# Round 1's first retention head: both projection quads in turn, in seven block products, with a changed release of the state work, in a split-precision conv and retention trunk

## The chip, the cores and the metric

One core of one Trainium2 chip. The metric is the device time of one execution in microseconds; for the kernel before it is the median of three runs. A program profiled once gives the trace that the readings below come from.

## The reference

One mixer layer on 2048 positions of 1024 features, with 16 learned meta tokens ahead of them. Every position is normalised and multiplied by one matrix of 1024 x 4096, and the result is cut into eight groups of 512: four feed a gated convolution of width three, four a retention with four heads of 128. Both halves are gated, joined and multiplied by a second matrix of 1024 x 1024, and a residual and a final normalisation follow.

```python
h = jnp.concatenate([meta_b, x], axis=1)
hn = rms_norm(h, norm_g)
proj = jnp.einsum('bld,de->ble', hn, w_in)
cx, cb, cc, cg, q, k, v, rg = jnp.split(proj, N_PROJ, axis=-1)
conv_out = short_conv_branch(cx, cb, cc, conv_w) * jax.nn.silu(cg)
qf = rotary(q.reshape(shp).astype(jnp.float32), pos) * (RET_HEAD_DIM ** -0.5)
kf = rotary(k.reshape(shp).astype(jnp.float32), pos)
ret = head_group_norm(retention_chunkwise(qf, kf, vf), ret_norm_g)
ret_out = ret.astype(h.dtype) * jax.nn.silu(rg)
mixed = jnp.concatenate([conv_out, ret_out], axis=-1)
return h + jnp.einsum('ble,ed->bld', mixed, w_out)
```

In the retention, each chunk of 128 positions has scores of q with k, multiplied by a decay and applied to v, and adds what q reads from a running state of 128 x 128, which is multiplied by a chunk decay and gets k^T v of each chunk. The state starts from the meta tokens.

## The kernel before, in words

**Precision and products.** Every operand of the large products is split into a high and a low part (`split`, L113): ScalarE (ACT) writes the high part as a cast, VectorE (DVE) subtracts it from the source for the low part. A product of two blocks is then three matmuls per 128 rows: low weights by high data (`wl`, `mh`), high by low (`wh`, `ml`), high by high. A matmul of the large kind has a 128 x 128 weight and 512 columns.

**Quads.** The work of TensorE (PE) is cut into quads: four output blocks of 128 x 512 from 2 x 2 blocks of weights and of data. `quad` (L252) makes one in seven block products of twelve matmuls each (Strassen's scheme in Winograd's form: seven sums of weights, seven sums of data, and sums of the outputs). `quad_plain` (L309) makes it in eight, without sums. The sums of the weights for products 2 to 5 are built by GpSimd (POOL) in `stationary` (L143): L131 and L128 on tiles `ra` and `sa`, each followed by the split, a cast `wh` on ACT (L119) and a low part `wl` on DVE (L120). Only three pairs `wh`, `wl` are held at a time (`RING`).

**Rounds and units.** Two rounds of 1024 positions. A round has eight units of two quads each: units 0 to 3 are retention heads (`head`, L787: one quad for K and V, one for Q and the gate RG), 4 to 7 are convolution groups (`conv_group`, L646). Round 0 takes them in the order 4, 0, 1, 2, 3, 5, 6, 7, round 1 in the order 0 to 7; then `output` makes the second product. In round 1 the first head has the plain quad for K and V (L309), because the data's sums are still on their way from DRAM (`prepared`, L224), and the quad in seven for Q and RG.

**What a head does behind its quads.** Outputs of a quad come by `take`: a copy `tc` of a bank by ACT (L259), a sum from bank and copy by DVE (`kv`, `qg`, L128). K and Q are rotated in place by four DVE operations (`rotary`, L742 to L745). V and K are taken apart into 16-bit planes (`part`), transposed by a DMA and put together again (`join`, `join_keys`, ACT). Then follow, for two halves j of four chunks each: products of v and kd that update the state (PE at L895, DVE at L898), the scores (PE at L908), their decay `pm` (DVE at L910), the outputs (v by pm at L918, state by q at L919), statistics and normalisation. The turned outputs (`apart`) come back from a DMA one unit later and are multiplied with the gate (DVE at L948).

**The meta tokens.** In round 0, sixteen small matmuls (L506, `meta_products`) multiply the raw weights `ra` of the *next* unit by the meta tokens; four ACT copies (L512) bring them to `mk`. Since POOL builds the weight sums in the same `ra` tiles, it waits for them. `meta_state` (L525) then makes a head's starting state: two DVE sums, three products and one sum on `mk` (L128, L532, L533), one matmul (L536), one copy.

**What sets the order.** Each engine works through its queue in the order in which it was given. The order comes from a scheduler that simulates the program, and from `tc.issue_after(x)`, which keeps what is written inside it behind instruction x in the order. `head` ends with two such places: `next(sums)` (a step that makes sums for the next round) and `meta_state` are put behind `queried[0]`, the first rotation of q, which comes behind product 1 of the second quad. Its second rotation comes behind product 5.

**The row product.** In `take` of `conv_group` (L664 to L676), the gated input u is multiplied by a row factor, `u<-u,rr`, on DVE (L663).

## Time and profile before

| what | us |
|---|---|
| median of three runs (864.99 to 865.04) | 865.0 |
| the profiled execution | 865.38 |
| its span, first to last instruction | 863.6 |
| PE busy | 853.8 |
| DVE busy | 675.1 |
| ACT busy | 499.7 |
| POOL busy | 280.0 |
| round 1's first head, plain quad and quad in seven | 354.0 to 405.7 |

Times in the views are counted from the start of the span. A row of the chain or of a timeline gives start, length, engine, what is written from what is read, the line, and how many instructions the row groups (a small matmul in full precision counts twice). "Idle before" stands in brackets with what ended it. A matmul's own length of 0.39 us is longer than its pitch, since matmuls overlap; the pitch counts.

### The profile page before, as it was taken

The page shows a single profiled execution, that of the slowest core. Times are in us where ns is not written, and L with a number is a line of the kernel's source. Part 1 is how long each engine was busy: PE and PEld are TensorE (multiplying, and loading weights), DVE is VectorE, ACT ScalarE, POOL GpSimd, SP SyncE. Part 2 cuts the span into 40 slices and gives each one's busy share as a digit, 9 for nine tenths or more (in the row PEclk, how much of TensorE's full clock was granted, in tenths as well). Part 3 has the DMA queues.
Part 4 walks back from the last instruction along what each step waited for, and adds up shares of the span by engine and source line. Part 5 has one row for each costly group of instructions (what it writes and reads, how often), then busy time and mean ns, then how long its engine had stood idle before and what let it go on. Part 6 is the DMA issues. An engine that isn't in the chain of part 4 may idle for free.

```text
span 863.6 us, 12850 instructions
## 1 busy us (share of the span) xinstructions
PE 853.8 (99%) x4216; PEld 705.5 (82%) x4216; DVE 675.1 (78%) x1207; ACT 499.7 (58%) x901; POOL 280.0 (32%) x224
## 2 busy tenths in 40 slices
PE   9999999999999999999999999999999999999996
PEld 6778888878887778888888888888888878888885
DVE  6798989889897977979677787976655699766553
ACT  7775648474845554948284757544433475555553
POOL 0032332422245554110000002341312154777773
PEclk9999999999999999999999999999999999999999
DMA  9736257565777744966275657547334584455441
GB/s 323 245 122 171 91 148 213 143 190 184 183 239 236 244 147 159 340 197 171 74 183 175 162 190 173 180 135 256 99 120 122 199 326 146 159 172 178 150 134 74
DMA packets 141331, 154.43 MB, mean 179 GB/s; under 512 B 59920, under 2 KB 77904, under 8 KB 141264
## 3 DMA queue, kind: packets, MB, share of 16 engines
q1 hardware_dynamic: 140688, 153.21, 57.6%
q8 instruction: 33, 0.54, 0.3%
q10 hardware_dynamic: 576, 0.40, 0.1%
q14 instruction: 34, 0.28, 0.1%
HBM read 101.14 MB, written 39.85 MB: 163 GB/s over the span
## 4 chain that ended last, share of the span: by engine, by line
PE 95%; DVE 2%; DMA 1%; ACT 1%; issue 1%; ACTq 0%; POOLq 0%; DVEq 0%; SPq 0%
PE pj L252 76%; PE pj L333 5%; PE pj L309 5%; PE ms L919 2%; PE ms L908 2%; PE ms L918 2%; PE ms L895 2%; PE ms L506 1%; DMA w<-in_w_out 1%; DMA ra<-in_w_in 0%; DVE wl L120 0%; DVE qg L948 0%; DVE x L205 0%; PE ms L381 0%; DVE u L663 0%
## 5 line engine op out<-in xcount | busy, mean ns | idle before, releaser
L252 PE MATMUL pj<-mh,wl 128*128 128x512 f32 x1008 | 395.6, 392 | 1.9 <-DVE wl L120 1.1
L252 PE MATMUL pj<-mh,wh 128*128 128x512 f32 x1008 | 393.2, 390 | 0.0
L252 PE MATMUL pj<-ml,wh 128*128 128x512 f32 x1008 | 392.8, 390 | 0.0
L119 ACT CAST wh<-ra 128x512 fp32r<-128x512 f32 x229 | 142.2, 621 | 256.2 <-PE pj L252 220.0
L120 DVE TENSOR_TENSOR wl<-ra,wh 128x512 fp32r<-128x512 f32 x229 | 185.8, 813 | 64.2 <-ACT wh L119 62.3
L252 PEld LDWEIGHTS pj<-mh,wl 128*128 128x128 f32 x1008 | 189.3, 188 | 42.8 <-ACT wh L119 1.7
L252 PEld LDWEIGHTS pj<-mh,wh 128*128 128x128 f32 x1008 | 189.2, 188 | 39.3
L252 PEld LDWEIGHTS pj<-ml,wh 128*128 128x128 f32 x1008 | 189.3, 188 | 38.3
L131 POOL TENSOR_TENSOR ra<-ra 128x512 f32<-128x512 f32 x44 | 68.3, 1553 | 80.9 <-PE ms L506 38.7
L931 POOL TENSOR_TENSOR rp<-rs,neg_half 128x4 f32<-128x4 f32 x16 | 18.8, 1173 | 150.3 <-DVE rs L128 150.2
L259 ACT COPY tc<-pj 128x512 f32<-128x512 f32 x108 | 62.6, 580 | 0.1
L128 POOL TENSOR_TENSOR sa<-ra 128x512 f32<-128x512 f32 x22 | 32.5, 1480 | 55.8 <-DMA ra<-in_w_in 28.7
L994 DVE TENSOR_TENSOR yo<-pj,yo 128x512 f32<-128x512 f32 (+1 forms) x33 | 21.9, 672 | 24.3 <-PE pj L252 16.1
L131 POOL TENSOR_TENSOR ra<-sa,ra 128x512 f32<-128x512 f32 x22 | 30.4, 1380 | 30.9 <-DVE wl L120 21.1
L1005 POOL TENSOR_TENSOR z<-yo,final_g 128x512 f32<-128x512 f32 x16 | 26.4, 1651 | 19.5 <-DVE yo L994 19.5
L128 POOL TENSOR_TENSOR yo<-yo,tc 128x512 f32<-128x512 f32 x18 | 28.0, 1560 | 6.6 <-ACT tc L259 6.5
L128 DVE TENSOR_TENSOR tc<-pj,tc 128x512 f32<-128x512 f32 x26 | 17.8, 686 | 15.4 <-PE pj L252 15.3
L935 DVE TENSOR_SCALAR pm<-ms,mv,rp 128x128 f32<-128x128 f32 x64 | 21.9, 403 | 10.1 <-POOL rp L931 10.0
L663 POOL TENSOR_TENSOR c<-c,tc 128x512 f32<-128x512 f32 x12 | 18.2, 1516 | 34.2 <-ACT tc L693 21.8
L663 POOL TENSOR_TENSOR c<-c,rr 128x512 f32<-128x512 f32 x12 | 19.3, 1609 | 27.1 <-DVE c L713 17.0
L581 DVE SCALAR_TENSOR_TENSOR c<-u,conv_w,c 128x512 f32<-128x512 f32 x32 | 25.2, 831 | 2.3 <-POOL u L572 1.2
L123 DVE SCALAR_TENSOR_TENSOR ml<-x,gain,mh 128x512 fp32r<-128x512 f32 x32 | 22.6, 745 | 4.7 <-ACT mh L122 4.7
(168 smaller groups left out, 1214.5 us busy)
## 6 DMA issues: line engine op xcount, KB each, us to landing
ra<-in_w_in SPq DMA_DIRECT2D x111, 256.0 KB, 2.9
ra<-sums_a SPq DMA_DIRECT2D x52, 256.0 KB, 2.9
x<-in_xT SPq DMA_DIRECT2D x48, 256.0 KB, 5.0
sums_a<-ra SPq DMA_DIRECT2D x42, 256.0 KB, 2.1
w<-in_w_out SPq DMA_DIRECT2D x32, 256.0 KB, 5.0
ra<-mixed SPq DMA_DIRECT2D x32, 256.0 KB, 2.7
yo<-in_x SPq DMA_DIRECT2D x32, 256.0 KB, 4.3
ra<-in_x SPq DMA_DIRECT2D x16, 256.0 KB, 3.3
```

Of the source, the lines that this page charges most:

```text
L119: nc.scalar.copy(out=hi, in_=src)
L120: lowered[0] = eng.tensor_tensor(out=lo, in0=src, in1=hi.bitcast(F32), op=ALU.subtract)
L123: nc.vector.scalar_tensor_tensor(out=lo, in0=src, scalar=scale, in1=hi.bitcast(F32), op0=ALU.mult, op1=ALU.subtract)
L128: eng.tensor_tensor(out=out, in0=a, in1=b, op=ALU.add)
L131: eng.tensor_tensor(out=out, in0=a, in1=b, op=ALU.subtract)
L252: nc.tensor.matmul(bank, a[:, ks], b, start=first and kt == 0 and n == 0, stop=kt == KH - 1 and n == 2, skip_group_check=not first,)
L259: copied[0] = nc.scalar.copy(out=c, in_=bank)
L309: nc.tensor.matmul(banks[i], a[:, ks], b, start=half + kt + n == 0, stop=half == 1 and kt == KH - 1 and n == 2,)
L333: nc.tensor.matmul(banks[n][i], a[:, ks], b, start=half + kt + s == 0, stop=half == 1 and kt == KH - 1 and s == 2,)
L581: nc.vector.scalar_tensor_tensor(out=c, in0=u[:, tap : tap + HB], scalar=conv_w[:, g, tap : tap + 1], in1=c, op0=ALU.mult, op1=ALU.add)
L663: eng.tensor_tensor(out=out, in0=a, in1=b, op=ALU.mult)
L1005: nc.gpsimd.tensor_tensor(out=ys[i][j], in0=y, in1=final_g[:, j * HB : (j + 1) * HB], op=ALU.mult)
```

## The change

Four things are changed.

1. Round 1's first head. A new `quads` makes both quads in turn: product 0 of K/V, product 0 of Q/RG, product 1 of K/V and so on, seven each (168 matmuls in place of 180). The weights of both come from generators (`weights_in_turn`) that load, cast and split one weight at a time in that order; a product's successor is asked for when the pair is issued. The data come by `moving_in_turn`: blocks, then the sums in the order 1, 0, 2, block B22, sum 3, as steps between the products. The sum T3 is split ahead of the two first rotations, which are put off (`turns`); B22 and T4 stand behind low parts of weights (`leads`). K's and V's transposes are no longer held back (`to_cross` is gone).
2. In round 0, `conv_group`'s row product for j = 0 stands behind the low part of the quad's fifth weights (`fifth`), where work of a head before it is still waiting.
3. In `take_queries`, the rotation is noted in `queried` only for j = 1.
4. `next(sums)` and `meta_state` stand behind `queried[-1]` in place of `queried[0]`. This holds for all heads of round 0 as well.

```diff
+    def quads(ws, w, m, takes, between=()):
+        between = iter(between)
+        banks = [[None, None] for _ in ws]
+        copies = [None for _ in ws]
...
+        for i in range(7):
+            for n in range(len(ws)):
+                if i < 2:
+                    banks[n][i] = ps_proj()
+                product(n, i, banks[n][i in (1, 3, 5)], i in (0, 1, 3))
+            w = [next(a, None) for a in ws[:1]]
+            leads[0] = lowered[0]
+            w += [next(a, None) for a in ws[1:]]
...
+            next(between, idle)()
...
+    def weights_in_turn(n, r):
+        for load in w_loads(n, r, in_line):
+            a = raw()
+            load(a)
+            yield weight_parts(a)
...
+        behind_head = r == 0 and len(waiting[1]) + len(waiting[0]) > 0
...
-                mul(nc.vector, s, s, rr2[j])
+                with queued((fifth[0],) if behind_head and j == 0 else ()):
+                    mul(nc.vector, s, s, rr2[j])
...
-                rotary(d, tables[j])
-                queried.append(turned[0])
+                if j == 0 and len(first):
+                    turns.append(lambda: rotary(d, tables[j]))
+                else:
+                    rotary(d, tables[j])
+                if j:
+                    queried.append(turned[0])
...
+            steps = [
+                first[1], lambda: turn_first(early[0]), fourth, fifth_pair, lambda: turn_first(leads[0]), split_values,
+                lambda: split_keys(1),
+            ]
+            quads(*first[0], m, (take_keys, take_queries), steps)
+            join_keys(0)
+            join(1)
+            weigh(1)
+            join(0)
+            weigh(0)
+            join_keys(1)
...
-        with tc.issue_after(queried[0].ins):
+        with tc.issue_after(queried[-1].ins):
             next(sums, None)
         if blocks[1]:
-            with tc.issue_after(queried[0].ins):
+            with tc.issue_after(queried[-1].ins):
                 meta_state(h, blocks[1], rot)
```

The order of PE in round 0, from head 1 to head 2, before: the head's starting state, the next head's meta products and the first state update stand right behind product 6's matmuls (the first row), and the next unit's product 0 follows (the last row).

```order
L252 MATMUL pj<-mh_461,wl 128x512
L252 MATMUL pj<-ml_462,wh 128x512
L252 MATMUL pj<-mh_461,wh 128x512
L536 MATMUL ms<-mk 128x128
L506 MATMUL ms<-ra,meta_s 16x128 x16
L895 MATMUL ms<-v,kd 128x128 x4
L252 MATMUL pj<-mh_126,wl 128x512
```

After, the same place: these are the last matmuls of the next unit's product 1 (rows of L274, which is the old L252; L607, L577, L1002, L1015, L1025 and L1026 are the old L536, L506, L895, L908, L918 and L919).

```order
L274 MATMUL pj<-ml_223,wh 128x512
L274 MATMUL pj<-mh_222,wh 128x512
L607 MATMUL ms<-mk 128x128
L577 MATMUL ms<-ra,meta_s 16x128 x16
L1002 MATMUL ms<-v,kd 128x128 x8
L1015 MATMUL ms<-qg,kv 128x128 x4
L1025 MATMUL ms<-v,pm 128x128
L1026 MATMUL ms<-state_84,qg 128x128
L1025 MATMUL ms<-v,pm 128x128
L1026 MATMUL ms<-state,qg 128x128
L1025 MATMUL ms<-v,pm 128x128
L1026 MATMUL ms<-state,qg 128x128
```

The block moved behind two products of the next unit, in one piece, and the scores with the first outputs moved up to it; behind the rows shown come the rest of the outputs, the second scores and the next unit's product 2.

The order of DVE in round 0, from head 0 to head 1, before: the operations on `mk` follow the first rotation of q (whose last operation is the first row).

```order
L745 TENSOR_TENSOR qg<-qg,rot 128x512
L128 TENSOR_TENSOR mk<-mk 16x128 x2
L533 TENSOR_TENSOR mk<-mk,mr 16x128
L532 TENSOR_TENSOR mk<-mk,mr 16x64 x2
L120 TENSOR_TENSOR wl<-ra,wh 128x512
L128 TENSOR_TENSOR mk<-mk 16x128
L128 TENSOR_TENSOR qg<-pj,tc 128x512
L837 TENSOR_TENSOR qg<-qg,rr 128x512
```

After: here the second rotation of q begins the rows (L821 to L824 are the old L742 to L745, L671 is the old L594, L604 and L603 the old L533 and L532).

```order
L821 TENSOR_TENSOR rot<-qg,rot_t 64x512
L822 TENSOR_TENSOR rot<-qg,rot_t 64x512
L908 TENSOR_TENSOR qg<-pj,rr 128x512
L823 TENSOR_TENSOR qg<-qg,rot_t 128x512
L824 TENSOR_TENSOR qg<-qg,rot 128x512
L671 TENSOR_TENSOR c<-c,rr 128x512 x2
L128 TENSOR_TENSOR mk<-mk 16x128 x2
L671 TENSOR_TENSOR c<-c,cb 128x512 x2
L604 TENSOR_TENSOR mk<-mk,mr 16x128
L603 TENSOR_TENSOR mk<-mk,mr 16x64 x2
L671 TENSOR_TENSOR c<-c,cb 128x512 x2
L128 TENSOR_TENSOR mk<-mk 16x128
```

The operations on `mk` moved behind the second rotation and between the products on c, which belong to the unit before.

The order of DVE in round 0 at conv unit 6's first quad, before (the row of L663 is the row product):

```order
L120 TENSOR_TENSOR wl<-sa,wh 128x512
L948 SCALAR_TENSOR_TENSOR qg<-apart,ret_g,qg 128x512
L128 TENSOR_TENSOR u<-pj,tc 128x512
L948 SCALAR_TENSOR_TENSOR qg<-apart,ret_g,qg 128x512
L663 TENSOR_TENSOR u<-u,rr_360 128x512
L120 TENSOR_TENSOR wl<-ra,wh 128x512 x3
L128 TENSOR_TENSOR ss<-ss 128x4
```

After:

```order
L120 TENSOR_TENSOR wl<-sa,wh 128x512
L1055 SCALAR_TENSOR_TENSOR qg<-apart,ret_g,qg 128x512
L128 TENSOR_TENSOR u<-pj,tc 128x512
L1055 SCALAR_TENSOR_TENSOR qg<-apart,ret_g,qg 128x512
L120 TENSOR_TENSOR wl<-ra,wh 128x512
L741 TENSOR_TENSOR u<-u,rr_360 128x512
L120 TENSOR_TENSOR wl<-ra,wh 128x512 x2
L128 TENSOR_TENSOR ss<-ss 128x4
```

One `wl`, the low part of the fifth weights, moved ahead of the row product (the old L663, now L741).

## The prediction

> **What bounds the kernel now.** I read the page first, then PE's waits, then the chain of work that ended last.

> ```profile
> span 863.6 us, 12850 instructions
> PE 853.8 (99%) x4216; PEld 705.5 (82%) x4216; DVE 675.1 (78%) x1207; ACT 499.7 (58%) x901; POOL 280.0 (32%) x224
> PEclk9999999999999999999999999999999999999999
> ```

> TensorE (PE) is busy for 99% of the span at the full granted clock. A matmul taken out is worth its own time, and a new wait on PE is paid in full. PE's waits hold one entry above 1 us inside the units:

> ```profile
> PE pj L252 <- DVE wl L120: 1.1, 1, 1.1
> ```

> The chain through round 1's first head (K/V quad at L309, Q/RG quad at L252) is matmuls without a gap:

> ```profile
> 354.03 5.44 PE pj L252 x24
> ...
> 370.58 16.09 PE pj L309 x71
> 386.67 19.04 PE pj L252 x84
> 405.71 0.89 PE ms L895 x8
> ```

> 84 matmuls take 19.04 us, 0.2267 us each, and L309 runs at the same pitch (16.09/71). A product of twelve is 2.72 us.

> **Part 1: seven products for eight in round 1's first head.** 96 + 84 matmuls become 84 + 84: 12 x 0.2267 = -2.72 us. What covers the new work is the slack of the other engines. The window of the two old quads (columns: length, then busy PE, weight loads, DVE, ACT, POOL):

> ```profile
> 354.00:405.70 51.70, 51.70 (x231) 42.81 (x230) 45.09 (x72) 38.32 (x66) 3.46 (x2) 1.00 0.76 244
> ```

> The K/V quad gains three low parts of weights and three sums on DVE, at 0.6 to 0.7 us each (rows below), about 4 us: 45.1 + 4 = 49.1 in a window of 51.7 - 2.7 = 49.0. DVE just fits; ACT, with three casts and three copies more (some 3.6 us), has room. Two quads in turn give each weight two products (5.44 us) of lead, and the rotations are put off, so DVE can slide. I count no stall, with 0 to +2 us as bounds: nothing in the trace makes it a gain, and if the cover is gone PE waits for a low part of one weight, priced as in part 2 at 1 to 2 us.

> **Part 2: the row product.** Columns: start, length, what, idle before it.

> ```profile
> 294.62 0.39 PE L252 MATMUL pj<-mh,wh 128*128 128x512 f32 x1
> 296.08 0.47 PE L252 MATMUL pj<-mh,wl 128*128 128x512 f32 x1 [1.07 <-DVE wl L120]
> ```

> ```profile
> 293.54 1.79 DVE L663 TENSOR_TENSOR u<-u,rr 128x512 f32<-128x512 f32 x1
> 295.25 1.88 DVE L120 TENSOR_TENSOR wl<-ra,wh 128x512 fp32r<-128x512 f32 x3
> ```

> In conv unit 6 DVE runs the row product ahead of the fifth weights' low part, and PE starts 296.08 - 294.62 - 0.23 = 1.23 us late. The new order puts the low part first: it can start at 293.54 instead of 295.25, 1.71 us sooner, which covers the 1.23. I take -1.2; bounds 0 (something else ends the wait) and -1.24.

> **Part 3: what `queried` moves in round 0.** The change appends only the second rotation of q and ties `meta_state` and `next(sums)` to it. That holds for every head, not only round 1's first. The order shows the result: in round 0, for heads 0, 1, 2 and 3, PE's block "meta state, 16 meta products, v by kd, scores" now stands behind products 0 and 1 of the next unit, directly ahead of product 2. Before, it was spread from product 5 on:

> ```profile
> 90.59 0.41 PE ms L536 x2
> 91.01 0.56 PE ms L506 x16
> 91.57 2.99 PE pj L252 x12
> 94.55 0.56 PE ms L506 x16
> 95.11 1.09 PE ms L895 x8
> ...
> 101.21 0.89 PE ms L895 x8
> 102.10 0.89 PE ms L908 x8
> ...
> 141.01 1.00 PE ms L506 x32
> ```

> Gain: where the meta products were in two pieces (heads 0 and 2) they cost 2 x 0.56 + (2.99 - 2.72) = 1.39 us, in one piece 1.00. Twice 0.39 is -0.8 us (bounds 0 and -0.8).

> Cost: what had other matmuls to hide behind now stands at one place, where PE itself waits. Behind the meta products the block holds only 1.09 + 0.89 + 0.89 = 2.87 us of PE work before product 2.

> *Head 0 to 1, the wait for `mk`.* PE is through product 5 at 90.59; 36 matmuls later, 8.16 us, it stands at the block: 98.7. The prices of DVE's rows there:

> ```profile
> 94.56 0.69 DVE L742 TENSOR_TENSOR rot<-qg,rot_t 64x512 f32<-64x512 f32 x1
> 95.27 1.82 DVE L743 TENSOR_TENSOR rot<-qg,rot_t 64x512 f32<-64x512 f32 x1
> 97.11 0.69 DVE L837 TENSOR_TENSOR qg<-pj,rr 128x512 f32<-128x512 f32 x1
> 97.72 0.28 DVE L898 SCALAR_TENSOR_TENSOR state<-state,ms 128x128 f32<-128x128 f32 x1
> ...
> 100.41 1.28 DVE L594 TENSOR_TENSOR c<-c,rr 128x512 f32<-128x512 f32 x2
> 101.61 0.28 DVE L898 SCALAR_TENSOR_TENSOR state<-state,ms 128x128 f32<-128x128 f32 x1
> ```

> ```profile
> 85.35 0.47 DVE L128 TENSOR_TENSOR mk<-mk 16x128 f32<-16x128 f32 x2
> ...
> 86.33 0.69 DVE L120 TENSOR_TENSOR wl<-ra,wh 128x512 fp32r<-128x512 f32 x1
> 86.94 0.27 DVE L128 TENSOR_TENSOR mk<-mk 16x128 f32<-16x128 f32 x1
> ```

> From 94.56 on, DVE has in its new order, counted from start to start: two rotation halves 1.42; gate by row factor 0.61, rotation's product 0.60 and sum 0.71; c by rr, two, 1.20; four products c by cb at the same pitch, 2.40; the mk operations 0.98 and 0.27. Together 8.2, so mk is there at about 102.7 and PE waits 4.0 us (3.7 to 4.3: each of the ten operations may be some 0.03 us off).

> *Head 0 to 1, product 2.* Its weights (third in line) are built by POOL from tiles that the meta products still read, and DVE must first finish what the block feeds:

> ```profile
> 95.26 1.28 POOL L131 TENSOR_TENSOR ra<-ra 128x512 f32<-128x512 f32 x1 [13.84 <-PE ms L506]
> 96.61 1.62 POOL L131 TENSOR_TENSOR ra<-sa,ra 128x512 f32<-128x512 f32 x1
> ```

> ```profile
> 95.21 1.06 ACT L512 COPY mk<-ms 16x128 f32<-16x128 f32 x4 [1.13 <-PE ms L506]
> 98.27 0.62 ACT L119 CAST wh<-ra 128x512 fp32r<-128x512 f32 x1 [0.82 <-POOL ra L131]
> 99.63 0.59 ACT L259 COPY tc<-pj 128x512 f32<-128x512 f32 x1
> ```

> By POOL: meta products' end 95.11 to the cast 98.27 is 3.16, cast 0.62, low part 0.69: 4.5. By ACT and DVE: mk copies 0.10 + 1.06, copy tc 0.59, then kv sum 0.67, state 0.28, two rotation halves 1.40, state 0.28, low part 0.69: 5.0. Against 2.87 of PE work the wait is 2.2 us. POOL runs beside it, and the row 95.27 shows what that does: 1.82 us for a rotation half whose twin took 0.69. One such meeting adds 1.1, two 2. I take 3.0 (2.2 to 4.2). [...]

> *Heads 1 to 2 and 2 to 3.* Here even the outputs of j = 0 (v by pm, state by qg) stand in the block, so PE waits for pm:

> ```profile
> 197.29 0.74 DVE L948 SCALAR_TENSOR_TENSOR qg<-apart,ret_g,qg 128x512 f32<-128x512 f32 x1
> 197.95 0.27 DVE L898 SCALAR_TENSOR_TENSOR state<-state,ms 128x128 f32<-128x128 f32 x1
> ...
> 198.81 0.68 DVE L910 SCALAR_TENSOR_TENSOR pm<-ms,causal 128x512 f32<-128x512 f32 x1
> 199.41 0.67 DVE L128 TENSOR_TENSOR kv<-pj,tc 128x512 f32<-128x512 f32 x1
> ```

> mk copies and tc 1.75, kv 0.67, state 0.27, rotation half 0.70, gate 0.74, other half 0.69, state 0.2, pm 0.68: with overlaps at the seams about 5.5; less 2.87 is 2.65 each. One meeting with POOL makes it 3.75. I take 3.3 each (2.65 to 3.75).

> *Head 3 to conv unit 5.* mk copies 1.16, DVE's mk work of the conv unit 0.74, states 0.7, u's sum 0.6, gate 0.7, pm 0.68: 4.6 less 2.87; I take 2.3 with part of a meeting (1.7 to 2.8).

> Sum of waits: 4.0 + 3.0 + 3.3 + 3.3 + 2.3 = +15.9, bounds 12.9 and 18.8.

> **The sum.** -2.7 - 1.2 - 0.8 + 15.9 = +11.2. The profiled execution took 865.38 us (its span and 1.8 outside); the median of the runs is 865.0, so the execution stands 0.4 above it, and the same step on the median gives 876. Bounds: 12.9 - 4.8 = +8.1 (873) to 18.8 - 2.7 + 0 + 2 - 0.8 = +17.3 (882).

> **Rivals.**
> 1. *Faster: the waits are covered.* Mechanism: the mk and pm chains are ready when PE gets there. It decides at the point where mk is done before 98.7 and the chain behind the meta products takes under 2.87 us. For it: before, these steps never made PE wait. Against: then about thirty full matmuls stood between scores and their use, now none. Time: 865.0 - 4.8 = 860.2.
> 2. *Half of it.* DVE fills PE's first wait with work that I counted behind it, and each later wait shrinks: +8 - 4.8 = +3, 868 (866.8 to 873).
> 3. *The clock.* Idle time lowers PE's granted clock. The only longer idle in the trace is the start:

> ```profile
> 0.99 4.45 PE L1070 MATMUL ms<-warm 128*128 128x512 bf16 x10 [0.99 <-DVE warm L1062]
> ```

> Ten matmuls take 0.445 us each, twice the later 0.2267: a cold stretch costs 2.2 us. After one wait of 4.0 that is 878; after all four of 3 us and more, 885. Against: after the wait of 1.07 us PEclk is unchanged. [...]
> 4. *Same.* Waits of about 5 us in all cancel the gains: 863.3 to 866.7.

> **Chances.** 0.2% is 1.7 us, about what a measurement of this kernel can tell from no change. Waits as summed 0.62; clock 0.10; half 0.08; covered 0.16; same 0.04. So slower 0.80, same 0.04, faster 0.16. Predicted: 876, the likeliest case, alone 873 to 882. The range runs from 864 to 882: it leaves out the covered case and the far end of the clock's.

> **What would show it.** In the new profile: no PE gap between 354 and 406 (part 1), with the next head's first small matmuls 2.7 us nearer to the first head's start; no wait of PE on wl near conv unit 6 (part 2); in round 0 four times a PE wait on mk, wl or pm directly ahead of a third product, 2 to 4 us each and two at head 0 to 1 (part 3). Wrong it is if PE's waits in round 0 sum to under 5 us, or if the first waits of round 1's first head exceed 2 us.

## The result and the profile after

The changed kernel takes 887.2 us (median; 886.6 to 887.8) against 865.0 before: 22.2 us slower, ratio 1.0253 (95% interval 1.0240 to 1.0266). The direction and the place were as forecast, the size was double: 876 was predicted, with 882 as the upper end of the range.

The page of the kernel after, with the lines that answer to those of before:

```profile
span 884.8 us, 12809 instructions
PE 859.6 (97%) x4204; PEld 711.6 (80%) x4204; DVE 688.0 (78%) x1209; ACT 498.8 (56%) x901; POOL 275.3 (31%) x224
PEclk9999899998999999999999999999999999999999
```

PE has twelve matmuls fewer and yet is busy 5.8 us longer, and two of the forty digits of the granted clock have fallen. So there are two costs: idle time, and matmuls that run slowly. The idle time is in PE's waits (us in total, times, longest):

```profile
PE ms L1025 <- DVE pm L1017: 8.0, 2, 4.0
PE ms L607 <- DVE mk L128: 3.6, 1, 3.6
PE ms L1025 <- ACT wh L119: 2.9, 1, 2.9
PE pj L274 <- DVE wl L120: 1.9, 1, 1.9
...
PE pj L274 <- ACT wh L119: 0.7, 1, 0.7
```

The first four rows are the five waits that the prediction named, 16.4 us together. The third row's wait is also one of v by pm; the page lists a cast as its last releaser.

The chain from head 0 to head 1 shows both costs in one place:

```profile
101.99 0.21 DVE mk L128
102.20 0.04 issue
102.25 0.79 PE ms L607 x2
103.04 1.91 PE ms L577 x32
104.95 0.02 issue
104.97 0.26 ACT mk L583
...
106.05 0.59 ACT tc L281
106.64 0.02 issue
106.67 0.69 DVE kv L128
107.36 0.20 DVE state L1005
107.58 0.69 DVE rot L821
108.28 1.68 DVE rot L822
109.98 0.29 DVE state L1005
110.27 0.61 DVE wl L120
110.88 0.04 issue
110.93 5.73 PE pj L274 x24
```

mk comes at 102.20, forecast 102.7. Behind the block stands the path that was added up by hand (mk copies, copy tc, kv, state, two rotation halves, state, low part), with one half at 1.68 us, beside a POOL operation (107.73 to 109.41), where the other took 0.69. But the matmul on mk takes 0.79 us, before 0.41, and the 32 records of the meta products 1.91 us, before 1.00: the granted clock is 0.50 there. The windows behind the long waits give the granted clock (the column behind the five engines):

```profile
102.25:104.00 1.75, 1.75 (x22) 1.32 (x26) 0.00 (x0) 0.27 (x1) 0.00 (x0) 0.50 0.95 268
104.00:106.00 2.00, 2.00 (x25) 1.53 (x14) 0.00 (x0) 0.99 (x4) 0.98 (x1) 0.50 0.10 27
106.00:108.00 2.00, 2.00 (x14) 2.00 (x13) 1.30 (x3) 0.94 (x3) 1.84 (x3) 0.63 0.35 131
```

```profile
162.00:164.00 2.00, 1.93 (x9) 1.96 (x10) 2.00 (x4) 0.00 (x0) 0.00 (x0) 0.52 0.59 206
164.00:165.50 1.50, 1.50 (x9) 1.50 (x9) 1.50 (x4) 0.00 (x0) 0.00 (x0) 0.50 0.77 239
```

```profile
214.80:217.00 2.20, 2.19 (x10) 2.20 (x11) 2.20 (x4) 0.00 (x0) 0.00 (x0) 0.50 0.60 203
217.00:219.00 2.00, 2.00 (x12) 2.00 (x11) 1.33 (x5) 0.00 (x0) 0.17 (x1) 0.50 0.73 174
219.00:221.00 2.00, 2.00 (x10) 1.84 (x10) 2.00 (x6) 0.00 (x0) 1.92 (x2) 0.72 0.42 130
```

```profile
267.30:269.00 1.70, 1.69 (x10) 1.70 (x11) 1.70 (x4) 0.02 (x1) 0.00 (x0) 0.68 1.00 310
269.00:271.00 2.00, 2.00 (x12) 2.00 (x11) 2.00 (x7) 0.00 (x0) 0.00 (x0) 0.50 0.85 251
271.00:272.00 1.00, 1.00 (x8) 0.96 (x8) 0.76 (x5) 0.00 (x0) 0.00 (x0) 0.85 0.58 180
```

Length times the missing share of the clock is 2.6, 1.7, 2.7 and 1.7 us: 8.7 us in all. It shows in the busy time too: twelve matmuls fewer should have made it 2.7 us shorter, and it is 5.8 us longer.

Over the whole kernel, here is how late the same large matmul starts in the changed kernel's trace against the trace of before, at eight places (counted in matmuls of 512 columns from the start; twelve fewer behind the first head of round 1):

| large matmul | place | us later than before |
|---|---|---|
| 350th | head 0, ahead of its end | -0.5 |
| 450th | head 1 under way | +7.8 |
| 640th | head 2 under way | +13.6 |
| 790th | head 3 under way | +19.9 |
| 950th | conv unit 5 under way | +25.1 |
| 1150th | conv unit 6 under way, behind its wait | +24.4 |
| 1665th | round 1's second head under way | +21.8 |
| the 3400th | output | +21.1 |

The four heads cost 8.2, 5.8, 6.4 and 5.1 us, 25.5 in all; waits and clock make 16.4 + 8.7 = 25.1 of it. The first head of round 1 gives 2.6 back, as forecast. The -0.5 of the first row is there from the second matmul on and is not the change's doing: at the start the clock rose at 5.07 us in this trace and at 6.06 us in that of before.

### The profile page after: what moved, and what is told of

The parts are those of the page before. It is cut to its first block, busy times and chain, and to the rows that moved or that the text cites. A ratio compares the mean times of both kernels' runs of the same rounds, so it can differ in the third digit from the quotient of the medians.

```text
span 884.8 us, 12809 instructions
## 1 busy us (share of the span) xinstructions
PE 859.6 (97%) x4204; PEld 711.6 (80%) x4204; DVE 688.0 (78%) x1209; ACT 498.8 (56%) x901; POOL 275.3 (31%) x224
## 4 chain that ended last, share of the span: by engine, by line
PE 91%; DVE 4%; ACT 2%; DMA 1%; issue 1%; SPq 0%; POOL 0%; POOLq 0%; DVEq 0%; ACTq 0%
PE pj L274 71%; PE pj L404 5%; PE pj L322 4%; PE pj L380 2%; PE ms L1025 2%; PE ms L1026 2%; PE ms L1015 1%; PE ms L577 1%; PE ms L1002 1%; ACT wh L119 1%; DMA w<-in_w_out 1%; DVE rot L822 1%; DMA ra<-in_w_in 1%; PE ms L1177 0%; ACT mk L583 0%
## 5 line engine op out<-in xcount | busy, mean ns | idle before, releaser
L274 PE MATMUL pj<-mh,wl 128*128 128x512 f32 x980 | 384.7, 393 | 2.8 <-DVE wl L120 1.9
L274 PE MATMUL pj<-mh,wh 128*128 128x512 f32 x980 | 381.9, 390 | 0.0
L274 PE MATMUL pj<-ml,wh 128*128 128x512 f32 x980 | 381.5, 389 | 0.0
L119 ACT CAST wh<-ra 128x512 fp32r<-128x512 f32 x236 | 146.5, 621 | 265.1 <-PE pj L274 200.8
L120 DVE TENSOR_TENSOR wl<-ra,wh 128x512 fp32r<-128x512 f32 x236 | 196.0, 832 | 63.5 <-ACT wh L119 62.4
L274 PEld LDWEIGHTS pj<-mh,wl 128*128 128x128 f32 x980 | 184.2, 188 | 42.7 <-DVE wl L120 2.1
L274 PEld LDWEIGHTS pj<-mh,wh 128*128 128x128 f32 x980 | 184.0, 188 | 38.6
L274 PEld LDWEIGHTS pj<-ml,wh 128*128 128x128 f32 x980 | 184.1, 188 | 37.2
L131 POOL TENSOR_TENSOR ra<-ra 128x512 f32<-128x512 f32 x44 | 67.3, 1530 | 107.8 <-PE ms L577 79.1
L128 POOL TENSOR_TENSOR sa<-ra 128x512 f32<-128x512 f32 x22 | 30.6, 1392 | 65.0 <-DMA ra<-in_w_in 30.6
L131 POOL TENSOR_TENSOR ra<-sa,ra 128x512 f32<-128x512 f32 x22 | 30.3, 1379 | 27.8 <-DVE wl L120 17.6
L1025 PE MATMUL ms<-v,pm 128*128 128x128 f32 x128 | 27.7, 301 | 10.9 <-DVE pm L1017 8.0
L1025 PEld LDWEIGHTS ms<-v,pm 128*128 128x128 f32 x128 | 22.8, 213 | 12.3 <-issue 8.3
L1042 DVE TENSOR_SCALAR pm<-ms,mv,rp 128x128 f32<-128x128 f32 x64 | 21.8, 404 | 11.3 <-POOL rp L1038 11.3
L128 DVE TENSOR_TENSOR tc<-pj,tc 128x512 f32<-128x512 f32 x26 | 17.8, 686 | 15.9 <-PE pj L274 15.8
L741 POOL TENSOR_TENSOR c<-c,tc 128x512 f32<-128x512 f32 x12 | 18.8, 1570 | 31.6 <-ACT tc L772 30.0
L128 POOL TENSOR_TENSOR yo<-yo,tc 128x512 f32<-128x512 f32 x18 | 26.5, 1481 | 3.5 <-ACT tc L281 3.2
L1026 PE MATMUL ms<-state,qg 128*128 128x128 f32 x128 | 27.4, 299 | 0.0
```

What stands on the lines that cost most here:

```text
L119: nc.scalar.copy(out=hi, in_=src)
L120: lowered[0] = eng.tensor_tensor(out=lo, in0=src, in1=hi.bitcast(F32), op=ALU.subtract)
L128: eng.tensor_tensor(out=out, in0=a, in1=b, op=ALU.add)
L131: eng.tensor_tensor(out=out, in0=a, in1=b, op=ALU.subtract)
L274: nc.tensor.matmul(bank, a[:, ks], b, start=first and kt == 0 and n == 0, stop=kt == KH - 1 and n == 2, skip_group_check=not first,)
L1025: nc.tensor.matmul(o[:, cs], pm[:, cs], vt[j][:, cs], start=True, stop=False)
```

## The experiments

**1. The state work put back.** Everything of the change but the release of the state work in round 0:

```diff
-                if j:
+                if j or not len(first):
                     queried.append(turned[0])
...
-        with tc.issue_after(queried[-1].ins):
+        with tc.issue_after(queried[0].ins):
             next(sums, None)
         if blocks[1]:
-            with tc.issue_after(queried[-1].ins):
+            with tc.issue_after(queried[0].ins):
                 meta_state(h, blocks[1], rot)
```

> Seven products in round 1's first head and the row product as in the changed kernel, but meta_state and next(sums) of round 0 back behind the first rotation of q. Theory (all of the loss is the moved state work: 16.4 us of PE waits and some 9 us of a lowered clock behind them): no PE wait of 1 us or more in round 0's heads, clock 0.998, 861.5 to 862.6 us (865.0 - 2.5 - 0.4). Rival (the first head's rework or the row product carries part of the loss): above 866 us.

Measured: 863.5 us beside 864.9 for before, ratio 0.9984 (0.9975 to 0.9993); clock 0.998, no wait of 1 us or more in round 0. The loss is gone, and the rival with it. The gain is smaller than expected; PE's waits show a new one:

```profile
PE pj L274 <- ACT tc L281: 1.1, 1, 1.1
```

ACT's timeline at the start of round 1's second head shows how it comes about:

```profile
406.48 1.35 ACT L930 COPY v<-tr 128x1024 uint16<-128x1024 uint16 x1 [1.35 <-DMA tr<-pl]
407.69 0.61 ACT L119 CAST wh<-ra 128x512 fp32r<-128x512 f32 x1
408.20 0.58 ACT L281 COPY tc<-pj 128x512 f32<-128x512 f32 x1
```

ACT stands at v's join until its transposing DMA has landed (5.30 us in the chain), and the cast and the copy tc that PE needs are queued behind it. With both quads in turn, v's last block comes out of the very last product of its quad, and its transposition has nothing left to hide behind.

**2. The late release alone,** on the kernel before:

```diff
-                queried.append(turned[0])
+                if j:
+                    queried.append(turned[0])
```

> The kernel before with only the noting of the second rotation: meta_state and next(sums) behind it in all heads of round 0. Theory: the whole loss without the rest, 889 to 891 us (865.0 + 25), clock about 0.987, waits on mk, wl, pm, pm, pm as in the changed kernel. Rival (the loss needs the new first head): 865 to 870 us.

Measured: 891.3 us, ratio 1.0323 (1.0301 to 1.0345), clock 0.987, the same five waits and one more of 1.3 us on a copy. One condition in one line makes the whole loss.

**3. The row product alone,** on the kernel before:

```diff
+        behind_head = r == 0 and len(waiting[1]) + len(waiting[0]) > 0
...
-                mul(nc.vector, s, s, rr2[j])
+                with queued((fifth[0],) if behind_head and j == 0 else ()):
+                    mul(nc.vector, s, s, rr2[j])
```

> The kernel before with only the row product behind the fifth weights' low part. Prediction's part 2: 863.8 us (-1.2), no wait before conv unit 6's product 4. By the trace of the changed kernel, where a wait on a cast wh (0.66 us, 0.82 us over the pitch) stands near there: -0.4, 864.6 us. Rival (the wait only moves): 865.0 us.

Measured: 864.6 us beside 864.9, ratio 0.9997 (0.9988 to 1.0006): by the times, not told from no change. In the trace the wait of unit 6 is gone and the same matmul behind it starts 1.3 us earlier, where the changed kernel gained 0.4. DVE in this kernel, and then in that of experiment 1:

```profile
291.28 0.74 DVE L950 SCALAR_TENSOR_TENSOR qg<-apart,ret_g,qg 128x512 f32<-128x512 f32 x1
292.00 1.72 DVE L120 TENSOR_TENSOR wl<-ra,wh 128x512 fp32r<-128x512 f32 x1
293.64 1.79 DVE L664 TENSOR_TENSOR u<-u,rr 128x512 f32<-128x512 f32 x1
```

```profile
291.62 1.80 DVE L1055 SCALAR_TENSOR_TENSOR qg<-apart,ret_g,qg 128x512 f32<-128x512 f32 x1
293.35 1.78 DVE L120 TENSOR_TENSOR wl<-ra,wh 128x512 fp32r<-128x512 f32 x1
295.05 0.68 DVE L741 TENSOR_TENSOR u<-u,rr 128x512 f32<-128x512 f32 x1
```

Two of these operations in turn take 1.7 to 1.8 us in place of 0.7, while POOL makes the next weights' sums beside them. Which two differs: in the first kernel POOL's first sum, which waits for a DMA, starts at 291.31 us, 0.03 us behind the gate, and the gate takes 0.74; in the second it starts at 291.58, 0.04 us ahead of the gate, and the gate takes 1.80. So there the gate ahead of the low part is long, and the low part starts 1.35 us later, which eats most of the gain.

**4. The sums' release put back, the state's left late.** As experiment 1, with only `next(sums)` behind `queried[0]`.

> The changed kernel with next(sums) alone back behind the first rotation of q; meta_state stays behind the second. Theory A (meta_state's place in the order carries the loss): 886 to 888 us, the same five waits. Theory B (the sums for round 1, which load DVE, POOL and the DMA queue, carry it): 862 to 866 us.

Measured: 887.6 us, ratio 1.0264 (1.0250 to 1.0278), waits of 3.6, 1.6, 4.0, 4.0 and 2.9 us. That is theory A: it is the place of `meta_state`, not the sums.

**5 and 6. PE kept busy during the waits.** The scores of half 0 are made again, 12 or 3 matmuls, into the bank that the outputs overwrite:

```diff
             o = ps_misc()
+            if r == 0 and h > 0 and j == 0:
+                for n in range(12):
+                    cs = slice(n % CH * P, (n % CH + 1) * P)
+                    nc.tensor.matmul(o[:, cs], k[0][:, cs], q[0][:, cs], start=True, stop=True)
```

> The changed kernel; behind the first scores of heads 1, 2 and 3 in round 0, PE makes 12 more score matmuls (2.7 us, results overwritten) while it would wait for pm; the second scores of heads 1 and 2 now also stand ahead of that wait (0.9 us each). PE's idle time there falls from 4.0, 4.0 and 2.9 us to some 0.4, 0.4 and 0.2. Theory (the idle time lowers the granted clock, which costs about 2 us more per head): v by pm and the scores behind the wait at full speed in heads 1 to 3, still at half behind head 0's mk wait; 887.2 - 1.8 - 6.1 = 879.3 us (878.3 to 880.3). Rival (the slow small matmuls come from standing together, not from idleness): 885.4 us.

> The same with 3 matmuls (0.67 us): about 2.4, 2.4 and 2.2 us of idle time are left. In the changed kernel 1.9 us of idle time left the clock as it was and 2.9 us lowered it. If what counts lies above 2.4 us: 879.3 us as with twelve. If it lies below 2.2: 885.4 us. Rival as before (not idleness): 885.4 us.

Measured: with twelve 881.4 us, ratio 1.0196 (1.0180 to 1.0212), clock 0.995; with three 882.1 us, ratio 1.0206 (1.0187 to 1.0224), clock 0.990. With more work on PE, the medians lie 5.8 and 5.1 us below the changed kernel's. These did not run beside it; in the traces, twelve more matmuls in each of three heads bring conv unit 6 forward by 5.7 us. With twelve, PE's waits in heads 1 and 2 are 0.6 us, and the clock stays at 1.00 behind them (161.7 to 165.0 and 213.0 to 216.0): the clock's part came back (5.8 of the 6.1 expected), the 1.8 us for the second scores did not, since these had to wait for the state sums themselves. With three, PE's waits on the second product's low part and on the state sums of heads 1 and 2 were:

```profile
110.96 0.66 PE L274 MATMUL pj<-mh,wl 128*128 128x512 f32 x1 [1.81 <-DVE wl L120]
...
163.05 0.38 PE L1015 MATMUL ms<-qg,kv 128*128 128x128 f32 x1 [2.64 <-DVE state L1005]
...
213.51 0.79 PE L1015 MATMUL ms<-qg,kv 128*128 128x128 f32 x2 [2.64 <-DVE state L1005]
```

A wait of 2.64 us left the clock alone once and halved it once. One of 2.10 us on pm in head 3 left it alone (granted clock 1.00 from 265.0 to 267.0), and yet one of 1.81 us halved it. So idleness is the cause (with twelve matmuls in these waits the clock stayed at 1.00), and the length of a wait alone does not say whether it counts. The expectation had two cases for this and the run gave a third.

Where the idle time falls tells the two waits of 2.64 us apart. In the changed kernel's trace the granted clock rises first at 5.07 us, falls to half at 100.64, 162.08, 213.28 and 267.89 us and is back at 107.47, 165.49, 220.11 and 271.31: 28, 46, 61 and 77, and 30, 47, 63 and 78 steps of 3.413 us behind that first rise. Here are the steps of that length in experiment 6's trace at the three waits, each with the step behind it (the first number behind the length is PE's busy time, the column behind the five engines the granted clock):

```profile
107.73:111.14 3.41, 1.60 (x14) 1.41 (x13) 3.37 (x5) 1.62 (x3) 1.69 (x1) 1.00 0.45 169
111.14:114.56 3.42, 3.42 (x9) 2.64 (x10) 3.39 (x8) 0.00 (x0) 0.77 (x1) 0.50 0.43 111
158.93:162.34 3.41, 1.48 (x14) 1.28 (x12) 3.31 (x5) 3.41 (x5) 2.40 (x2) 1.00 0.43 159
162.34:165.76 3.42, 2.71 (x25) 2.71 (x25) 3.39 (x7) 0.27 (x1) 0.00 (x0) 1.00 0.63 206
210.13:213.54 3.41, 0.77 (x8) 0.58 (x6) 3.31 (x5) 2.94 (x5) 1.70 (x1) 1.00 0.29 106
213.54:216.96 3.42, 3.42 (x16) 3.42 (x17) 3.42 (x7) 0.00 (x0) 0.00 (x0) 0.50 0.67 217
```

The first wait of 2.64 us straddles a border, with 1.93 us of idle time in one step and 0.71 in the next; the second lies in one step whole. In the changed kernel's trace these are the steps at full clock with more than 1.1 us of idle time, ahead of its last microseconds:

```profile
97.23:100.64 3.41, 1.42 (x7) 0.84 (x5) 3.41 (x10) 0.00 (x0) 0.00 (x0) 1.00 0.00 0
107.47:110.88 3.41, 1.54 (x14) 1.35 (x12) 3.33 (x6) 1.66 (x3) 1.86 (x2) 1.00 0.51 192
158.67:162.08 3.41, 0.01 (x1) 0.04 (x1) 3.35 (x5) 2.26 (x4) 1.07 (x1) 1.00 0.50 167
209.87:213.28 3.41, 0.94 (x9) 0.75 (x7) 3.31 (x5) 3.41 (x5) 2.52 (x2) 1.00 0.41 154
264.48:267.89 3.41, 0.58 (x5) 0.61 (x6) 3.41 (x8) 2.84 (x5) 1.28 (x1) 1.00 0.40 137
```

The next step was at half behind 1.99, 3.40, 2.47 and 2.83 us of idle time here and behind 1.81 and 2.64 in experiment 6; it was at full clock behind 1.87 us here and behind 1.93 there. So a wait of 2.64 us cost a step at half clock or nothing, by where it fell; why 1.81 us counted and 1.87 and 1.93 did not is not shown.

**7. v's join behind the next copy.** On the kernel of experiment 1: the join of v's half 0 and the state work that needs it are given out in the next head, behind its first copy of a bank.

```diff
             join(1)
             weigh(1)
-            join(0)
-            weigh(0)
             join_keys(1)
...
+        def state_work():
+            if len(first):
+                join(0)
+                weigh(0)
...
+        if len(first):
+            waiting[1].append(state_work)
+        else:
+            state_work()
```

> The version with round 0's state work back, and in round 1's first head v's join of half 0 (which waits for a transposing DMA of 5.3 us) and the state work behind it are given out behind the next head's first copy of a bank; ACT's order has the cast and that copy ahead of the join. Theory (the first head gives part of its 2.7 us back because ACT stands at the join, and the next head's copy is queued behind it): no PE wait on a copy tc at the start of round 1's second head, 861.5 to 862.3 us, or 1.2 us below the version without this. Rival (the wait moves to the values by keys or to pm): as that version, 863.5 us.

Measured: 862.3 us beside 864.6 for before, ratio 0.9971 (0.9960 to 0.9981): faster than the kernel before, by 0.3%. ACT now has the copy ahead of the join, and PE does not wait for it:

```profile
406.43 0.62 ACT L119 CAST wh<-ra 128x512 fp32r<-128x512 f32 x1
406.95 0.58 ACT L281 COPY tc<-pj 128x512 f32<-128x512 f32 x1
407.46 1.36 ACT L930 COPY v<-tr 128x1024 uint16<-128x1024 uint16 x1
```

In the traces the first head gains 1.2 us in experiment 1 and 2.65 us here, nearly the whole of the twelve matmuls. The times agree as to sign; the two kernels did not run beside each other, and their intervals overlap in part, so the gain over experiment 1 rests on the traces.

**8 and 9. One head at a time.** The kernel of experiment 1 with `queried[-1 if h == 0 else 0]` for `meta_state`, and the same with `h == 1`.

> The version with round 0's state work back behind the first rotation, except head 0, whose meta_state stays behind the second. Theory (each head's waits and its stretch of lowered clock stand by themselves): PE waits 3.6 us on mk and 1.9 on the low part of product 2's weights, then half clock for about 5 us; +8.2 over the version without, 871.7 us (863.5 + 8.2), of which the prediction had priced 7.0 - 0.4. Rival (the waits of one head come from what the head before left late): under 868 us.

> The same with head 1 alone behind the second rotation. Theory: one wait of 4.0 us on pm and 1.7 us lost by the clock, +4.6 to +5.8 over the version with all put back, 868.1 to 869.3 us. Rival (the 4.0 us of head 1 come from head 0's lateness): under 866 us.

Measured: head 0 alone 869.7 us, ratio 1.0058 (1.0040 to 1.0076); head 1 alone 869.3 us, ratio 1.0061 (1.0042 to 1.0080). Head 0 has its waits of 3.6 and 1.5 us and costs 7.1 us in the trace, in place of 8.2: here one step at half clock followed the waits (1.7 us lost), in the changed kernel two (2.6). The time is 2 us below the one expected. Head 1 has its wait of 4.0 us and costs 5.6 us, 1.6 of it by the clock, as expected. No head needs another's lateness: the rivals of both fall.

## Why the prediction was wrong, point by point

**Part 1** (-2.7): -2.6 in the changed kernel's trace. "I count no stall" held there. In experiment 1 a stall of 1.1 us did come, within the bound of 2, though not where the bound had put it (a weight's low part) but on a copy behind v's join.

**Part 2** (-1.2): -0.4. The prediction took only the low part's earlier start. The row product was not long by itself: at 293.54 it stood beside a POOL operation (293.15 to 294.78 in the trace of before), and the low part, put there, is long in its place (1.78 us in the changed kernel, 0.69 when alone). With that length it would have ended at 295.3 in place of 295.9, some 0.6 us sooner by estimate, not 1.71. A gate of 1.47 us (0.74 in experiment 3), beside POOL's sum from 316.83 to 318.12, stood ahead of it as well.

**Part 3, the gain** (-0.8): about -0.3, in head 2 alone. There the meta products in one piece took 1.07 us in place of 1.39; in head 0 they took 1.91 us at half clock, more than two pieces would.

**Part 3, the waits** (+15.9): 16.4 measured. Term by term, forecast and measured: mk 4.0 and 3.6, product 2 of head 1 3.0 and 1.9, the two waits on pm 3.3 and 4.0 each, the last 2.3 and 2.9. The mechanism was right in each place. That the sum agrees is in part luck: all five lie outside their own bounds, two below and three above, and the errors cancel. Product 2 waited less because its path (6.0 us, from 104.95 to 110.93) ran beside a block that itself took longer at half clock: PE's 2.87 us of work there became 4.0.

**The step that failed** is the sum's missing term, "Rivals, 3. The clock": the sum has the waits alone, and the runs showed 8.7 us of half clock behind them. Its price was nearly right, 2.2 us for each cold stretch and 885 for four; there were four, of 2.2 us on average (1.7 to 2.7). That the count came out is partly luck: the rival counted the waits forecast at 3 us and more, but product 2's came out at 1.9 us and left the clock alone, while the last, forecast at 2.3, came out at 2.9 and halved it. The term was held to one chance in ten and kept out of the sum. The reason given against it, that the clock was unchanged after a wait of 1.07 us, bears on waits of that length only. The waits forecast were two to four times as long, and the one slow stretch that it showed, the start (0.445 us for a matmul in place of 0.2267), spoke for the drop. With the clock the prediction would have been 876 + 8.8 = 885; most of the rest, to 887.2, is what parts 2 and 3 did not gain (0.8 + 0.5) and the waits' extra 0.5.

The upper end of the range has a slip as well: it takes the gain of 0.8 as sure, though its own bound for it is 0. Without it the end is 883, still far below the time measured.

The two rivals on the other side fell: nothing covered the waits, and DVE did not use the first wait to shorten the later ones.

## What to carry to other kernels

An order hint that is moved for one place holds wherever its line runs: read the new order of each engine at every such place, and look for a block of small operations that now stands alone at a place where the engine itself waits. In the changed kernel's heads the waits on PE, 2.9 to 4.0 us and one of 1.9, cost themselves and 1.7 to 2.7 us a head more by the clock; for waits of 1.81 to 2.64 us, those of experiment 6 among them, the clock's part came in some cases and not in others. A copy that waits for a DMA shouldn't stand ahead of one that the bottleneck waits for, on an engine that takes its queue in order: in experiment 1 it made PE wait 1.1 us.
